# A two-layer hybrid attention backbone in fp32: the second score product of two head groups over all 128 array rows, with half of key's low part zero

## The chip, the cores and the metric

The kernel runs on one core of one Trainium2 chip. The metric is the device time of one launch in microseconds (us), the median of several runs. Less is better.

## What is computed

Two layers; each normalises 256 context tokens and 512 latent tokens of width 1024, projects them with one wide input matrix, and runs three head groups beside each other: neighbourhood attention (N, 8 heads of 64), latent attention with compressed query and key (M, 8 heads of 96) and differential attention (D, 4 heads, each with two softmax maps of 64). Every branch is gated, projected, merged and projected once more.

```python
s = jnp.einsum('bqhd,bkhd->bhqk', q, k).astype(jnp.float32) * scale      # M
s = jnp.einsum('bqhmd,bkhmd->bhmqk', q, k).astype(jnp.float32) * scale   # D
s_lat = jnp.einsum('bnqhd,bnkhd->bhnqk', qr, kb).astype(jnp.float32) * NA_SCALE + bias  # N, window
s_ctx = jnp.einsum('bnqhd,bkhd->bhnqk', qr, k_ctx).astype(jnp.float32) * NA_SCALE       # N, context
```

Everything is fp32. The kernel makes each fp32 product out of products of a high part `hi` (rounded to fp32r) and the rest `lo = x - hi`: `hi*hi + hi*lo + lo*hi`.

## The kernel before

`mixer` (L867) runs a layer as 12 steps in the order `DMNDMNDMNDMN`; each step projects one pair of heads of the kind named and computes the attention of the pair projected in the step before. Beside them stand work units with no hurry: gate products (`zgate` and `gm`, in the PSUM tile `fl`) and the modulation products (`ada_rows`, L230). The instructions of all this are put in order, engine by engine, by a scheduler that goes by the priorities in `PRI` and by its own times for the instructions, so TensorE's queue mixes score products of one pair with the projections of the next and with gate work, and each engine takes its queue strictly from the front.

**Projection of N and D pairs.** `proj_nd` (L398) computes q, k and v of two 64-wide heads `m = 0, 1` for tiles of 128 tokens (`mm3`, L115 to L117, in PSUM tile `pj`), normalises, and transposes (L451). Head 0 then lies on partitions 0 to 63 and head 1 on 64 to 127 (`halves`). For each head it keeps `q[m]`, 128 partitions with the high part of q in the head's own half and q's low part in the other half (L461, L462); `k[m]`, 128 partitions with the high part of k in the own half, which a DMA copies into the other half (L468); and the low part of k, `kl`, a tile of 128 partitions by 768 tokens in which head 0 has the upper and head 1 the lower 64 partitions. `kl` is written by VectorE in `split` (L127, D) or `gsplit` (L131, N); its tag has one buffer, and each projection of an N or D pair takes the tile anew.

**Scores of N and D.** A score tile takes two products (L470): `q[m]` by `k[m]` over 128 rows, which gives `qhi*khi + qlo*khi` at once, and `q[m][half]` by `kl[half]` over the 64 rows of the head, which gives `qhi*klo`:

```python
out["ops"] = lambda m, q0, k0, w: [(q[m][:, q0:q0 + P], k[m][:, k0:k0 + w]),
                                   (q[m][halves[m], q0:q0 + P], kl[halves[m], k0:k0 + w])]
```

`scores` (L690) issues the two one after the other: for D's latent queries over 512 and then 256 keys, 64 times in all (two layers, four pairs, two groups of 256 queries, two blocks of 128, two maps), and for context queries of D and N over 256 keys, 32 times in layer 0. `pair_scores` (L731), for latent N queries, issues for 256 context keys and again for 256 window keys the first products of both heads and then the second products of both: 8 products per call, 32 calls. M's scores use L690 too, with three products over 96 rows and no half tile.

**After the scores.** All scores go through one PSUM tile `sc` of 1024 columns (one buffer). VectorE takes the maximum (L796 for D), ScalarE the exponential (L694), after which `sc` is free again; N adds a bias first (L732). The probabilities are transposed (L680, L720) and multiplied with v (L851, L810).

Of the kernel before, what the change touches and what calls it, by code (L numbers as in the profile page):

```python
# [8 lines left out]
F32R = mybir.dt.float32r  # L9
# [5 lines left out]
P = 128  # L15
# [4 lines left out]
NTOK = CTX + SEQ  # L20
# [28 lines left out]
def f(ap):  # L49
    return ap.bitcast(F32)  # L50


class Mixer:
# [112 lines left out]
        nc.vector.tensor_scalar(out, ss, inv, EPS, ALU.mult, ALU.add)  # L166
        nc.gpsimd.tensor_tensor(out, out, self.nhalf[:, :cols], ALU.pow)  # L167

    # ---------------------------------------------------------------- setup
    def setup(self):  # L170
        nc, io = self.nc, self.io
        cc = self.cpool.tile([P, KT, 2], F32, name="cc")
        nc.sync.dma_start(cc, io["cc"])
        th = self.cpool.tile([P, KT, 2], F32, name="cth")
        nc.scalar.activation(th, cc, AF.Tanh, scale=0.5)
        nc.vector.scalar_tensor_tensor(th, th, 1.0, cc, ALU.add, ALU.mult)
        self.sT = self.cpool.tile([P, KT, 32], F32, name="sT")
        nc.gpsimd.memset(self.sT, 0.0)
        nc.vector.tensor_scalar(self.sT[:, :, 0:2], th, 0.5, None, ALU.mult)
        self.L = [self.layer_params(l) for l in range(DEPTH)]  # L180
# [124 lines left out]
            else:  # L305
                self.bg.pop(0)()

    # ---------------------------------------------------------------- h
    def norm_tile(self, pool, xt):
        nc = self.nc  # L310
        junk = pool.tile([P, D], F32, tag="junk", bufs=1, name=self.n("junk"))
        ss = self.lpool.tile([P, 1], F32, tag="ssx", bufs=6, name=self.n("ssx"))
        nc.scalar.activation(junk, xt, AF.Square, accum_out=ss)
        self.rstd(ss, ss, 1.0 / D, 1)
        nc.vector.tensor_scalar(xt, xt, ss, None, ALU.mult)
# [58 lines left out]
                nc.gpsimd.tensor_scalar(hi, tmp, 1.0, 0.0, ALU.mult, ALU.add)  # L374
                nc.vector.tensor_tensor(lo, tmp, f(hi), ALU.subtract)

    # ---------------------------------------------------------------- projections
    def proj_tok(self, ps, ws, t):
        for k in range(KT):
            a = [self.h[j][:, k, t * P:(t + 1) * P] for j in range(2)]  # L380
            self.mm3(ps, a, ws[k], k == 0, k == KT - 1)
# [16 lines left out]
    def proj_nd(self, l, kind, pr, pool, br):  # L398
        nc, io, Lp = self.nc, self.io, self.L[l]
        ws = self.units(io["w_qkv"][l, (0 if kind == "N" else 4) + pr])  # L400
        q, k = self.qks(pool), self.qks(pool)
        kl = pool.tile([P, NTOK], F32R, tag="kl", name=self.n("kl"))
        halves = (slice(0, 64), slice(64, 128))
        V = [pool.tile([P, 3, 256], F32R, tag="V", name=self.n("V")) for _ in range(2)]
        for tp in range(3):
            qks = []
            for t in (2 * tp, 2 * tp + 1):
                kv = l == 1 and t < 2
                o = P if kv else 0
                ng = 2 if kv else 4  # L410
                ps = self.pj()
                self.proj_tok(ps[:, o:384], [(a[:, o:], b[:, o:]) for a, b in ws], t)
                qn = pool.tile([P, 384], F32, tag="qn", name=self.n("qn"))
                one = self.ONE
                if one:
                    nc.scalar.copy(qn[:, o:], ps[:, o:384])
                    ps = qn
                self.vwrite(kind, V[t // 3][:, t % 3, :], ps[:, 256:384], one)
                v4 = lambda x: x[:, o:256].rearrange("p (a b) -> p a b", b=64)
                ss = pool.tile([P, 4], F32, tag="ss", name=self.n("ss"))  # L420
                r = ss[:, :ng].unsqueeze(2).to_broadcast([P, ng, 64])
                if kind in self.COPY or one:
                    if not one:
                        nc.scalar.copy(qn[:, o:256], ps[:, o:256])
                    sq = pool.tile([P, 256], F32, tag="sq", name=self.n("sq"))
                    nc.scalar.activation(sq[:, o:256], ps[:, o:256], AF.Square)
                    raw = qn
                else:
                    nc.scalar.activation(qn[:, o:256], ps[:, o:256], AF.Square)
                    sq, raw = qn, ps  # L430
                nc.vector.tensor_reduce(ss[:, :ng], v4(sq), AX.X, ALU.add)
                if kind == "D":
                    q3 = qn[:, o:256].rearrange("p (a m b) -> p a m b", m=2, b=64)
                    na = ng // 2
                    if t < 2:
                        nc.vector.tensor_tensor(q3, q3, br["G"][:, 2 - na:2].unsqueeze(2).to_broadcast([P, na, 2, 64]), ALU.mult)
                    else:
                        C, S = br["C"][:, t - 2], br["S"][:, t - 2]
                        t2 = pool.tile([P, 2, 2, 64], F32, tag="t2", name=self.n("t2"))
                        for x, y in ((0, 32), (32, 0)):  # L440
                            nc.gpsimd.tensor_tensor(t2[:, :, :, x:x + 32], q3[:, :, :, y:y + 32], S[:, :, x:x + 32].unsqueeze(2).to_broadcast([P, 2, 2, 32]), ALU.mult)
                        nc.vector.tensor_tensor(q3, q3, C.unsqueeze(2).to_broadcast([P, 2, 2, 64]), ALU.mult)
                        nc.vector.tensor_tensor(q3, q3, t2, ALU.add)
                self.rstd(ss[:, :ng], ss[:, :ng], 1.0 / 64, ng)
                nc.vector.tensor_tensor(v4(qn), v4(raw), r, ALU.mult)
                qks.append(qn)
            kv = l == 1 and tp == 0
            pt = self.pj()
            for i, qn in enumerate(qks):
                for j in ((1,) if kv else (0, 1)):  # L450
                    nc.tensor.transpose(pt[:, j * 256 + i * P:j * 256 + (i + 1) * P], qn[:, j * P:(j + 1) * P], self.ident)  # L451
            c = slice(tp * 256, tp * 256 + 256)
            if self.PF:
                pf = pool.tile([P, 512], F32, tag="pf", name=self.n("pf"))
                o = 256 if kv else 0
                (nc.scalar.copy if self.PF == "a" else nc.vector.tensor_copy)(pf[:, o:], pt[:, o:])
                pt = pf
            p3 = pt.rearrange("p (a t) -> p a t", a=2)
            for m, (own, oth) in enumerate((halves, halves[::-1])):
                if not kv:  # L460
                    nc.scalar.copy(q[m][own, c], p3[own, 0])  # L461
                    nc.vector.tensor_tensor(q[m][oth, c], p3[own, 0], f(q[m][own, c]), ALU.subtract)  # L462
                if kind == "N":
                    self.gsplit(k[m][own, c], kl[own, c], p3[own, 1], Lp["g"][own, 0:1])
                else:
                    self.split(k[m][own, c], kl[own, c], p3[own, 1])
        for m, (own, oth) in enumerate((halves, halves[::-1])):
            nc.sync.dma_start(f(k[m][oth, :]), f(k[m][own, :]))  # L468
        out = dict(V=V)
        out["ops"] = lambda m, q0, k0, w: [(q[m][:, q0:q0 + P], k[m][:, k0:k0 + w]),  # L470
                                           (q[m][halves[m], q0:q0 + P], kl[halves[m], k0:k0 + w])]
        if kind == "N":
            Vs = br["pool"].tile([P, 3, 256], F32R, tag="Vs", name=self.n("Vs"))
            nc.sync.dma_start(f(Vs[0:64, 0, :]), f(V[0][64:128, 2, :]))
            nc.sync.dma_start(f(Vs[0:64, 1:3, :]), f(V[1][64:128, 0:2, :]))
            nc.sync.dma_start(f(Vs[64:128, :, :]), f(V[1][0:64, :, :]))
            out["Vs"] = Vs
            out["bias"] = []
            for ty in range(3):
                bt = br["pool"].tile([P, 2, 256], F32, tag="bias", name=self.n("bias"))  # L480
                nc.sync.dma_start(bt, self.biasd[l][ty][2 * pr:2 * pr + 2].rearrange("h p k -> p h k"))
                out["bias"].append(bt)
        return out
# [166 lines left out]
        out["ops"] = ops  # L650
        return out

    # ---------------------------------------------------------------- attention
    def attn(self, l, kind, pr, a, zs, pool, ud):
        for grp in (self.GRP if l == 0 else (1, 2)):
            self.attn_group(l, kind, a, zs, pool, ud[self.BI[kind], pr], grp)
# [197 lines left out]
        nc.scalar.copy(tmp[mine, :], o[other, 0:256])  # L854
        nc.vector.tensor_tensor(u[mine, :], o[mine, 0:256], tmp[mine, :], ALU.add)  # L855

    # ---------------------------------------------------------------- layer
    POOLS = dict(pt2=1, th=1, qn=2, sq=2, t2=2, c2=2, c3=2, kr=2, krt=2, mss=2, ssr=2, ss=2)
    BUFS = dict(pf=1, mr=1, qk=6, kl=1, V=5, P=3, pt4=4, pt2=2, zs=2, ut=3, sq=1, ss=4, qn=3, st=3, t2=1, r0=2, th=1, c2=2, c3=1, mss=4, krt=2, Vs=1, bias=1, kr=1, ssr=1)
    BI = {"N": 0, "M": 1, "D": 2}  # L860
# [6 lines left out]
    def mixer(self, l):  # L867
# [4 lines left out]
        pool = _Pool(ps, self.BUFS, self.POOLS)  # L872
        gms = list(range(24))
        ada = [(0, 4), (0, 5), (1, 2), (1, 0), (1, 3), (1, 1)] if l == 0 else [(1, 4), (1, 5)]
        self.base = tc.cur_priority
        br = {"D": self.dtab, "N": dict(pool=pool), "M": None}
        prev = None
        seen = dict(D=0, M=0, N=0)
        for step, kind in enumerate(self.ORDER[l]):
# [53 lines left out]
        for n in range(KT):  # L933
# [4 lines left out]
            for c0, w in self.cols(l):  # L938
                c = slice(c0, c0 + w)
# [228 lines left out]
```

## Time and profile before

| | |
|---|---|
| median of 3 runs | 2018.39 us (2012.0 to 2019.07) |
| span of the profiled execution, first to last instruction | 2015.7 us |
| TensorE matmul busy | 1962.4 us, 97% of the span |
| VectorE / ScalarE / GpSimd busy | 60% / 47% / 38% |
| TensorE's granted clock, mean | 0.990 of full speed |

The profiled execution's own time is given by its span alone; what lies around the span in a run isn't listed for it. The median of the runs is 2.7 us above that span, and the span lies between the fastest and the slowest of the runs.

In a timeline, a matmul's row gives its start and a modelled duration. Matmuls overlap, so what one costs TensorE's queue is the distance from its start to the next row's start, not its duration. PE is TensorE's matmul, DVE VectorE, ACT ScalarE, POOL GpSimd, SP the queue that issues transfers. "64*128" in a row of TensorE is rows by columns of the array in use.

### The profile page before, as it was taken

The numbers are of one execution on the slowest core, as the hardware profiler recorded it, in microseconds if no ns is written. First come the engines' busy times: TensorE is split into PE (matmuls) and PEld (weight loads), VectorE is DVE, ScalarE is ACT, GpSimd is POOL, SyncE is SP. The second block draws the span as 40 slices with busy tenths as digits, with TensorE's granted clock in tenths as the row PEclk, the third lists the DMA queues.
The fourth block names the chain that finished last, engine by engine and source line by source line (L and its number), as shares of the span: only waits on it lengthen the run. The fifth ranks groups of instructions, "written<-read, shape, count | busy, mean of one in ns | idle before, by whom it ended". The sixth has DMA issues, their size and how long they took to land.

```text
span 2015.7 us, 33972 instructions
## 1 busy us (share of the span) xinstructions
PE 1962.4 (97%) x11650; PEld 1745.5 (87%) x11650; DVE 1217.9 (60%) x2808; ACT 938.1 (47%) x2422; POOL 762.3 (38%) x1053
## 2 busy tenths in 40 slices
PE   6999999999999999999999999999999999999998
PEld 4988998998888988989999988897698789889878
DVE  5556667555765555646663465667667466666763
ACT  4445455444544544435532354555455345555531
POOL 3333233323423322332355454334344234343353
PEclk9999999999999999999999999999999899999999
DMA  9553113333434333332655243323513322432663
GB/s 320 185 157 123 41 56 104 110 120 111 124 110 145 90 100 119 98 108 70 199 175 178 92 129 125 110 66 91 163 54 93 112 72 81 119 126 59 189 188 112
DMA packets 172600, 243.28 MB, mean 121 GB/s; under 512 B 22710, under 2 KB 127560, under 8 KB 172428
## 3 DMA queue, kind: packets, MB, share of 16 engines
q1 hardware_dynamic: 172428, 241.12, 38.3%
q8 instruction: 92, 1.51, 0.3%
q14 instruction: 80, 0.66, 0.1%
HBM read 190.38 MB, written 44.49 MB: 117 GB/s over the span
## 4 chain that ended last, share of the span: by engine, by line
PE 90%; DVE 4%; DMA 2%; ACT 1%; issue 1%; POOL 1%; SPq 0%; DVEq 0%; ACTq 0%; POOLq 0%
PE pj L115 11%; PE pj L117 11%; PE pj L116 11%; PE fl L115 10%; PE fl L116 9%; PE fl L117 9%; PE sc L690 9%; PE bk L851 5%; PE bk L680 4%; PE fl L230 2%; PE sc L731 2%; PE bk L810 2%; PE pj L640 1%; PE pj L451 1%; DVE w L127 1%
## 5 line engine op out<-in xcount | busy, mean ns | idle before, releaser
L122 ACT CAST w<-ws 128x384 fp32r<-128x384 f32 (+3 forms) x520 | 237.2, 474 | 268.4 <-PE fl L116 159.2
L127 POOL TENSOR_TENSOR w<-ws,w 128x384 fp32r<-128x384 f32 (+3 forms) x260 | 241.9, 936 | 312.6 <-ACT w L122 301.7
L115 PE MATMUL fl<-h,w 128*128 128x384 f32 (+1 forms) x864 | 316.5, 366 | 4.1 <-DVE zs L392 2.7
L115 PE MATMUL pj<-w,h 128*128 128x384 f32 (+2 forms) x944 | 314.5, 336 | 2.0 <-DVE kl L127 1.1
L117 PE MATMUL fl<-h,w 128*128 128x384 f32 (+1 forms) x864 | 312.8, 362 | 0.0
L116 PE MATMUL fl<-h,w 128*128 128x384 f32 (+1 forms) x864 | 312.8, 362 | 0.0
L116 PE MATMUL pj<-w,h 128*128 128x384 f32 (+2 forms) x944 | 309.6, 330 | 0.0
L117 PE MATMUL pj<-w,h 128*128 128x384 f32 (+2 forms) x944 | 307.5, 330 | 1.0 <-POOL h L127 0.6
L127 DVE TENSOR_TENSOR w<-ws,w 128x384 fp32r<-128x384 f32 (+2 forms) x260 | 177.4, 686 | 74.4 <-ACT w L122 67.0
L167 POOL TENSOR_TENSOR ss<-ss,nhalf 128x4 f32<-128x4 f32 (+1 forms) x144 | 142.8, 992 | 179.2 <-DVE ss L166 166.3
L694 ACT ACTIVATE P<-sc,st 128x768 f32<-128x768 f32 (+1 forms) x192 | 159.5, 832 | 104.7 <-DVE st L796 39.1
L741 POOL TENSOR_SCALAR P<-P,st 128x512 f32<-128x512 f32 (+1 forms) x128 | 107.8, 845 | 256.0 <-DVE st L737 216.7
L684 DVE TENSOR_TENSOR pt<-bk,pt 128x512 fp32r<-128x512 f32 (+1 forms) x256 | 147.8, 586 | 64.9 <-ACT pt L683 62.7
L117 PEld LDWEIGHTS pj<-w,h 128*128 128x128 f32 x944 | 177.0, 189 | 9.6 <-issue 5.9
L115 PEld LDWEIGHTS pj<-w,h 128*128 128x128 f32 x944 | 177.6, 189 | 8.8 <-issue 3.8
L116 PEld LDWEIGHTS pj<-w,h 128*128 128x128 f32 x944 | 178.2, 189 | 5.7 <-issue 5.0
L115 PEld LDWEIGHTS fl<-h,w 128*128 128x128 f32 x864 | 164.4, 190 | 18.3 <-DVE zs L392 4.9
L117 PEld LDWEIGHTS fl<-h,w 128*128 128x128 f32 x864 | 164.1, 190 | 13.1 <-DVE w L127 0.5
L683 ACT CAST pt<-bk 128x512 fp32r<-128x512 f32 (+1 forms) x256 | 126.9, 506 | 104.3 <-PE bk L680 101.8
L116 PEld LDWEIGHTS fl<-h,w 128*128 128x128 f32 x864 | 164.2, 190 | 11.0
L690 PE MATMUL sc<-qk,qk 96*128 96x512 f32 (+3 forms) x592 | 153.2, 353 | 3.0 <-DMA qk<-qk 3.0
L680 PE MATMUL bk<-cst,P 128*128 128x128 f32 x832 | 130.1, 274 | 2.7 <-DVE u L855 1.8
(236 smaller groups left out, 3995.9 us busy)
## 6 DMA issues: line engine op xcount, KB each, us to landing
ws<-in_w_qkv SPq DMA_DIRECT2D x128, 192.0 KB
ws<-in_w_gm SPq DMA_DIRECT2D x96, 192.0 KB
aw<-in_w_ada SPq DMA_DIRECT2D x64, 256.0 KB
ct<-cqd SPq DMA_DIRECT2D x40, 384.0 KB
ct<-ckd SPq DMA_DIRECT2D x48, 256.0 KB
ws<-in_w_z SPq DMA_DIRECT2D x48, 192.0 KB
thd<-th SPq DMA_DIRECT2D x48, 192.0 KB
ws<-in_w_br SPq DMA_DIRECT2D x48, 192.0 KB
```

Source lines behind the costliest of these rows:

```text
L115: mm(out, a[0], b[0], start=first, stop=False)
L116: mm(out, a[0], b[1], start=False, stop=False)
L117: mm(out, a[1], b[0], start=False, stop=last)
L122: nc.scalar.copy(hi, src)
L127: (nc.gpsimd if le == "g" else nc.vector).tensor_tensor(lo, src, f(hi), ALU.subtract)
L167: nc.gpsimd.tensor_tensor(out, out, self.nhalf[:, :cols], ALU.pow)
L680: nc.tensor.transpose(pt[:, i * P:(i + 1) * P], src[:, (b0 + i) * P:(b0 + i + 1) * P], self.ident)
L683: nc.scalar.copy(h, v)
L684: nc.vector.tensor_tensor(lo, v, f(h), ALU.subtract)
L690: mm(s[:, d0:d0 + w], x, y, start=i == 0, stop=i == len(ops) - 1)
L694: nc.scalar.activation(p, src, AF.Exp, bias=st[:, m:m + 1], accum_out=st[:, 2 + m:3 + m])
L741: nc.gpsimd.tensor_scalar(p, p, st[:, 4 + m:5 + m], 0.0, ALU.mult, ALU.add)
```

## The change

The low part of k gets a tile of its own for each layer, `self.kl`, of 128 partitions by 2 heads by 768 tokens. At the start of the layer GpSimd sets the half that doesn't belong to the head to zero, in two memsets of 64 partitions by 768. Projections write the head's own half, as before, and the second product takes all 128 rows of `q[m]` and of `kl[:, m]`: q's low part, in the other half, meets zeros.

```diff
 def proj_nd(self, l, kind, pr, pool, br):
-        kl = pool.tile([P, NTOK], F32R, tag="kl", name=self.n("kl"))
+        kl = self.kl
...
                 if kind == "N":
-                    self.gsplit(k[m][own, c], kl[own, c], p3[own, 1], Lp["g"][own, 0:1])
+                    self.gsplit(k[m][own, c], kl[own, m, c], p3[own, 1], Lp["g"][own, 0:1])
                 else:
-                    self.split(k[m][own, c], kl[own, c], p3[own, 1])
+                    self.split(k[m][own, c], kl[own, m, c], p3[own, 1])
...
         out["ops"] = lambda m, q0, k0, w: [(q[m][:, q0:q0 + P], k[m][:, k0:k0 + w]),
-                                           (q[m][halves[m], q0:q0 + P], kl[halves[m], k0:k0 + w])]
+                                           (q[m][:, q0:q0 + P], kl[:, m, k0:k0 + w])]
...
 def mixer(self, l):
         br = {"D": self.dtab, "N": dict(pool=pool), "M": None}
+        self.kl = pool.tile([P, 2, NTOK], F32R, tag="kl", name=f"kl{l}")
+        for m in range(2):
+            self.nc.gpsimd.memset(f(self.kl[64 - 64 * m:128 - 64 * m, m]), 0.0)
```

Each engine issues the same instructions as before, apart from the four memsets on GpSimd. Their order shifts in places, because the tile is no longer taken anew by each pair and the scheduler plans again. Three places follow; a number behind a tile's name tells one tile of that name from another.

GpSimd at the start of layer 0, with the change: `h` is the normalised input, `mss` the mean squares of M's compressed inputs.

```order
L346 TENSOR_TENSOR h_1_109<-htmp_444,h_0_108 128x256
L346 TENSOR_TENSOR h_1_109<-htmp_460,h_0_108 128x512
L879 MEMSET kl_484 64x768 x2
L167 TENSOR_TENSOR mss_577<-mss_577,nhalf 128x1
L167 TENSOR_TENSOR mss_617<-mss_617,nhalf 128x1
```

The two memsets stand between the last piece of `h` and the first of the `mss` rows; those rows follow each other directly before. In layer 1 the pair of memsets stands between a piece of `h` and a weight's low part in the same way.

VectorE where layer 0 goes from its first N pair to its second D pair (step 3): `sc` with `bias` is the bias add on N's scores, `kl<-pj,qk` writes the low part of the D pair's keys. Before:

```order
L855 TENSOR_TENSOR u_3308<-bk_3381,ot_3394 64x256 [waits DMAHW0_49,Activation_49]
L855 TENSOR_TENSOR u_3308<-bk_3397,ot_3410 64x256 [waits Activation_49]
L732 TENSOR_TENSOR sc_3454<-sc_3454,bias_3174 128x2x256 [waits DMAHW1_49,PE_49]
L127 TENSOR_TENSOR kl_3572<-pj_3649,qk_3571 64x256
L127 TENSOR_TENSOR kl_3572<-pj_3744,qk_3571 64x256
```

With the change:

```order
L684 TENSOR_TENSOR pt_3311<-bk_3364,pt_3310 128x4x128 [waits Activation_49]
L127 TENSOR_TENSOR kl_484<-pj_3744,qk_3572 64x256 [waits PE_49]
L732 TENSOR_TENSOR sc_3421<-sc_3421,bias_3173 128x2x256 [waits PE_49]
L684 TENSOR_TENSOR pt_3313<-bk_3375,pt_3312 128x4x128 [waits Activation_49]
L501 TENSOR_TENSOR V_3574<-pj_3798,V_3574 128x128 [waits Activation_49]
```

Before, the D pair's first write of `kl` stands behind the last bias add of the N pair. Now it stands ahead of the bias add of the block before that one, and waits for TensorE itself.

TensorE in a later D pair of layer 0, around two successive score tiles `sc` of one block of queries. Before:

```order
L690 MATMUL sc_6604<-qk_6179,qk_6178 128x512
L690 MATMUL sc_6604<-kl_6180,qk_6178 128x512
L690 MATMUL sc_6604<-qk_6179,qk_6178 128x256
L690 MATMUL sc_6604<-kl_6180,qk_6178 128x256
L720 MATMUL bk_6563<-cst,P_6555 128x128 x4
L810 MATMUL bk_6570<-pt_6538,V_6181 128x256
L115 MATMUL fl_7247<-h_0_108,w_7229 128x384
```

With the change:

```order
L690 MATMUL sc_6602<-qk_6178,qk_6177 128x512
L690 MATMUL sc_6602<-kl_484,qk_6177 128x512
L690 MATMUL sc_6602<-qk_6178,qk_6177 128x256
L690 MATMUL sc_6602<-kl_484,qk_6177 128x256
L720 MATMUL bk_6561<-cst,P_6553 128x128 x4
L810 MATMUL bk_6568<-pt_6536,V_6179 128x256
L690 MATMUL sc_6610<-qk_6178,qk_6177 128x512
```

Before, twenty gate products (`fl`) and one transpose stood between these rows and the next score tile; with the change the next score tile follows after five short products.

## Rows read from the trace of the kernel before

**Rows 1.** The page: busy time per engine, and the chain that ended last

```profile
PE 1962.4 (97%) x11650; PEld 1745.5 (87%) x11650; DVE 1217.9 (60%) x2808; ACT 938.1 (47%) x2422; POOL 762.3 (38%) x1053
PE 90%; DVE 4%; DMA 2%; ACT 1%; issue 1%; POOL 1%; SPq 0%; DVEq 0%; ACTq 0%; POOLq 0%
```

**Rows 2.** Groups of TensorE by line, shapes apart: busy us, mean ns | idle before

```profile
L690 PE MATMUL sc<-kl,qk 64*128 64x256 f32 x96 | 36.8, 383 | 0.0
...
L690 PE MATMUL sc<-kl,qk 64*128 64x512 f32 x64 | 32.1, 501 | 0.0
...
L731 PE MATMUL sc<-kl,qk 64*128 64x256 f32 x128 | 25.6, 384 | 0.0
```

**Rows 3.** Timeline of TensorE, a D score tile: start us, us, instruction

```profile
185.03 0.39 PE L690 MATMUL sc<-qk,qk 128*128 128x512 f32 x1
185.35 0.50 PE L690 MATMUL sc<-kl,qk 64*128 64x512 f32 x1
185.78 0.38 PE L690 MATMUL sc<-qk,qk 128*128 128x256 f32 x1
186.09 0.39 PE L690 MATMUL sc<-kl,qk 64*128 64x256 f32 x1
186.41 0.44 PE L115 MATMUL fl<-h,w 128*128 128x384 f32 x1
186.69 0.33 PE L116 MATMUL fl<-h,w 128*128 128x384 f32 x1
186.86 0.34 PE L117 MATMUL fl<-h,w 128*128 128x384 f32 x1
```

**Rows 4.** Timeline of TensorE, value products and an M score tile

```profile
211.77 2.31 PE L810 MATMUL bk<-pt,V 128*128 128x256 f32 x18
213.92 1.21 PE L690 MATMUL sc<-qk,qk 96*128 96x512 f32 x6
214.96 0.34 PE L117 MATMUL pj<-w,h 128*128 128x384 f32 x1
215.14 0.34 PE L115 MATMUL pj<-w,h 128*128 128x384 f32 x1
```

**Rows 5.** Timeline of TensorE, one call of N's latent scores

```profile
285.68 0.48 PE L731 MATMUL sc<-qk,qk 128*128 128x256 f32 x2
286.09 0.38 PE L731 MATMUL sc<-kl,qk 64*128 64x256 f32 x2
286.40 0.50 PE L731 MATMUL sc<-qk,qk 128*128 128x256 f32 x2
...
287.15 0.44 PE L451 MATMUL pj<-cst,qn 128*128 128x128 f32 x2
```

**Rows 6.** Timeline of TensorE, three pairs of products of D's context queries

```profile
145.02 0.28 PE L690 MATMUL sc<-qk,qk 128*128 128x256 f32 x1
145.23 0.38 PE L690 MATMUL sc<-kl,qk 64*128 64x256 f32 x1
...
146.80 0.45 PE L115 MATMUL fl<-h,w 128*128 128x384 f32 x1
147.08 0.34 PE L116 MATMUL fl<-h,w 128*128 128x384 f32 x1
```

**Rows 7.** Who waited for whom, TensorE: us in total, times, longest us

```profile
PE pj L115 <- DVE kl L127: 1.1, 1, 1.1
```

**Rows 8.** Timelines of ScalarE and TensorE behind the D score tile of group 3

```profile
187.51 0.91 ACT L694 ACTIVATE P<-sc,st 128x768 f32<-128x768 f32 x1 [1.89 <-DVE st L796]
...
191.10 0.40 PE L690 MATMUL sc<-qk,qk 128*128 128x512 f32 x1
```

**Rows 9.** GpSimd: the nearest memset by tile, and its timeline as layer 0 starts

```profile
L74 POOL MEMSET neg<- x1: 311/311/311, 0.8 to 0.8; 128x256 f32 x1
...
49.84 1.33 POOL L346 TENSOR_TENSOR h<-htmp,h 128x512 fp32r<-128x512 f32 x1 [1.34 <-ACT h L344]
54.33 1.76 POOL L167 TENSOR_TENSOR mss<-mss,nhalf 128x1 f32<-128x1 f32 x3 [3.16 <-DVE mss L166]
```

## The prediction

> **What bounds the kernel.** I read the page first: matmuls keep TensorE busy for 97% of the span, VectorE, ScalarE and GpSimd for 60%, 47% and 38%, and 90% of the chain that ended last is TensorE's own work [rows 1]. What leaves TensorE's queue is therefore time, as long as nothing else is late. A busy share says nothing about how full the array is, so next come the groups of TensorE with the shapes apart. There, 288 products take only 64 rows of the array (96, 64 and 128 of them), and one over 256 columns is marked with 383 or 384 ns, over 512 with 501 [rows 2]. These durations overlap, so last I read the distances from start to start in the timeline.
>
> In a D score tile the starts lie at 185.03, 185.35, 185.78 and 186.09, and the gate product behind at 186.41: 1.38 us for two products of 512 and two of 256 columns; the next product is late too, 0.28 us instead of 0.17 [rows 3]. In an M score tile, which goes to the same `sc` and has 96 rows, three products of 512 and three of 256 columns take 1.04 us (the row counts all six and names the first one's shape), and behind them the distance is the usual 0.18 [rows 4]. The difference lies at every change between 128 and 64 rows: each product on either side of one starts some 0.1 to 0.2 us later than in a run of equal shapes.
>
> **Which form decides.** A 96-row product costs no more than one of full rows. The reading that fits all groups is that the array must be empty before it goes from a full-height to a half-height tile, or back. The Trainium skill, TensorEngine Tiling (Array Packing), Key Properties, says it so: changing the tiling mode drains the engine. The trace agrees, by the 1.38 us against two thirds of 1.04.
>
> **The sum, part by part.** All of it is distances on TensorE's queue, which is the path.
>
> 1. *D's latent scores, 64 tiles.* From 185.03 to 186.86 the queue does four score products and two gate products in 1.83 us [rows 3]. With full rows everywhere I take M's price: two thirds of 1.04, 0.69, plus two gate products at 0.18, 1.05 us [rows 4]. Gain 0.78 x 64 = 49.9 us.
> 2. *Context scores of D and N, 32 pairs of products.* Three pairs and one gate product take from 145.02 to 147.08, 2.06 us [rows 6]. Full products of 256 columns follow each other at (213.92 - 211.77) / 18 = 0.119 us [rows 4], so six and a gate product take 0.90. Gain 1.16 per three pairs, 0.39 x 32 = 12.4 us.
> 3. *N's latent scores, 32 calls of 8 products.* A call takes from 285.68 to 287.15, 1.47 us [rows 5]. Eight full products at 0.119 take 0.95. Gain 0.52 x 32 = 16.6 us. Here the change also gives something up: the second products of the two heads lie in different halves of the array, and both take only 0.31 us, 286.09 to 286.40 [rows 5]. Afterwards they stand one behind the other, which the 0.95 counts. The Trainium skill, TensorEngine Tiling (Array Packing), When to Use Tiling, speaks against the change: contractions of 64 or fewer rows are to be packed as two half tiles. By that rule alone padding would cost 64 more products of 0.119, 7.6 us, instead of bringing 16.6, and the sum of the three parts would be 54.7; I go by the rows, because in them the two changes of height cost more than the pairing saves.
>
> These make 78.9 us. Upper end: each call of N may also give back a late product behind it, as in D (0.1 x 32 = 3.2 us), and the one wait on a write of `kl`, 1.1 us [rows 7], may go: 83 us.
>
> 4. *Zero rows.* They cost TensorE nothing, since 96 rows cost what 128 do; VectorE writes as many partitions as before.
> 5. *Four memsets.* The nearest row is one of 256 columns, 0.31 us [rows 9]; 768 columns make 0.93, a pair 1.9 us per layer. In layer 0 GpSimd then idles 3.16 us before the `mss` rows [rows 9], which cover it. In layer 1 I don't know the cover: 0 to 1.9 us, and I take 0. Without cover M's first transposes would start that much later.
> 6. *The order.* At the seam from N to D, VectorE's first write of `kl` now stands ahead of a bias add and waits for TensorE. The waits for tokens that N's later blocks don't read end earlier, so PSUM tiles come free earlier; I count nothing. In a later D pair the next score tile follows after five short products, about 0.6 us. A score tile is free when the exponential has read it, 187.51 + 0.91 = 188.42, some 2.0 us behind its last product [rows 8]; so this place stalls by about 1.4 us. Elsewhere the next tile of the pair comes at 191.10 [rows 8], 2.7 us after the release. That distance consists of work that the change leaves alone, so the chain behind the scores is not squeezed where the order holds.
> 7. *What doesn't follow.* A tenth of the chain isn't TensorE's [rows 1], and in those stretches a shorter queue brings nothing: 78.9 x 0.1 = 7.9 us, an estimate. The 1.4 us of point 6 I count as part of it.
>
> Net gain 78.9 - 7.9 = 71 us. The profiled span is 2015.7, so the new span should be 1944.7. The median of the runs stands 2.7 us above that span, and I carry the same distance: **1947 us**, 3.5% less.
>
> **Rivals.**
>
> *Other engines become the bound.* TensorE gets ahead of weight splits and softmax steps, and waits take back 25 to 55 us, say half of 78.9. For it: VectorE would be busy 1217.9 of some 1945 us, 63%, and unevenly; one order place is tighter. Against: before, TensorE hardly waits on any of them, and the slack between score tiles holds filler that stays. Time 2018 - 40 = 1978 us; chance 0.14.
>
> *Only D gains.* If the pairing of half tiles is worth more in N than one call shows (in calls with other work between, the changes of height may be hidden), padding only adds 64 products of 0.119 there, and point 3 becomes a loss of 7.6 us: 49.9 + 12.4 - 7.6 = 54.7, less a tenth, 49. Time 2018 - 49 = 1969 us. The packing rule of the Trainium skill named in point 3 would have it so. The 1.47 us against 0.95 speak against it; chance 0.05.
>
> *The change doesn't do what it says.* If the late starts come from score operands or from `sc`, not from the array's height, the full-row second product keeps its distance, and N loses its pairs, 7.6 us: 2026 us, no change to speak of. M's scores have the same `sc` and the same 128-column operand at 1.04 us per six, which speaks against it; chance 0.04.
>
> *Slower, by the seam.* VectorE takes its queue in order. If the early `kl` write waits for TensorE while TensorE waits for something behind that write, each of the six seams from N to D becomes a stall. It decides only above 79 + 10 us, some 15 us at each seam, since the gain has to be eaten first; 20 us each would give 2018 - 71 + 120 = 2067. The wait that exists today there is 1.1 us, once [rows 7]. Chance 0.03.
>
> **How the numbers follow.** The forecast with its own ends (gain 55 to 90 us) has 0.74. The fast end is 83 us plus the spread of the runs shown, 7 us: 2018 - 90 = 1928. The slow end takes in most of the first rival and all of the second: 1984. About 0.5%, 10 us, is what a measurement of this kernel can tell from no change. Faster: forecast and the first two rivals, 0.93. The same: the third, and a little of the fourth that stays small, 0.04. Slower: 0.03.
>
> **What would show it.** Right: no group of 64 rows in TensorE's list, about 1.38 us shrunk to 0.7 in a D score tile and 1.47 to about 0.95 in an N call, the product behind at its usual 0.18; busy time of the other engines as before; TensorE's waits longer by under 10 us in all. Wrong: score products of full rows still 0.3 us apart (third rival); TensorE's waits on ScalarE and VectorE up by 25 us or more (first); a wait of `kl` on VectorE's queue with PSUM tiles held behind it (fourth).

## The result, and the profile after

The changed kernel takes **1949.18 us** (median of four runs, 1946.06 to 1951.95), the kernel before 2015.77 (four runs, 2012.0 to 2019.07): ratio 0.9666, 95% interval 0.9642 to 0.969, so 3.3% faster, 66.6 us. The forecast was 1947 in a range of 1928 to 1984. The profiled execution's own time is 1946.06 and its span 1944.3 us.

The page of the kernel after, busy time and chain, answers to [rows 1]:

```profile
PE 1882.9 (97%) x11650; PEld 1731.5 (89%) x11650; DVE 1213.2 (62%) x2808; ACT 936.3 (48%) x2422; POOL 766.0 (39%) x1057
PE 87%; DVE 4%; DMA 4%; ACT 2%; issue 1%; POOL 1%; SPq 0%; DVEq 0%; ACTq 0%; POOLq 0%
```

TensorE is 79.5 us less busy with the same 11650 products. It stands idle for 1944.3 - 1882.9 = 61.4 us, before for 2015.7 - 1962.4 = 53.3. The other engines' busy times hardly differ.

The groups of TensorE with shapes apart, kernel after, answer to [rows 2]:

```profile
L731 PE MATMUL sc<-kl,qk 128*128 128x256 f32 x128 | 26.8, 288 | 0.0
...
L690 PE MATMUL sc<-kl,qk 128*128 128x256 f32 x96 | 26.3, 281 | 0.0
...
L690 PE MATMUL sc<-kl,qk 128*128 128x512 f32 x64 | 25.1, 393 | 0.0
```

The same 288 products with `kl`, now all over 128 rows: over twice the rows each is marked shorter, 281 to 288 ns instead of 383 and 384, and 393 instead of 501. At a change of height a product's mark takes in the load of its weights, which starts with it there (last section); a shorter mark doesn't mean that a product computes faster.

The D score tile of [rows 3], timeline of TensorE, kernel after:

```profile
186.91 0.40 PE L690 MATMUL sc<-qk,qk 128*128 128x512 f32 x1
187.14 0.39 PE L690 MATMUL sc<-kl,qk 128*128 128x512 f32 x1
187.37 0.28 PE L690 MATMUL sc<-qk,qk 128*128 128x256 f32 x1
187.49 0.28 PE L690 MATMUL sc<-kl,qk 128*128 128x256 f32 x1
187.60 0.28 PE L117 MATMUL pj<-w,ct 128*128 128x256 f32 x1
```

From 186.91 to 187.60, 0.69 us instead of 1.38, and the product behind is followed at 187.72, the usual distance for 256 columns.

A call of N's latent scores, timeline of TensorE, kernel after, answers to [rows 5]; it stands behind transposes (L680), as the call of [rows 5] does:

```profile
278.22 0.38 PE L680 MATMUL bk<-cst,P 128*128 128x128 f32 x2
278.35 0.48 PE L731 MATMUL sc<-qk,qk 128*128 128x256 f32 x2
278.67 0.40 PE L731 MATMUL sc<-kl,qk 128*128 128x256 f32 x2
...
279.39 0.38 PE L451 MATMUL pj<-cst,qn 128*128 128x128 f32 x2
```

It takes 1.04 us instead of 1.47. The forecast was 0.95.

One view the prediction did not read says directly what went: the waits of the weight loads (PEld), where "issue" is a wait for nothing else that the profile shows. Columns: us in total, times, longest. Kernel before:

```profile
PEld sc L690 <- issue: 38.1, 137, 1.7
...
PEld sc L731 <- issue: 0.6, 3, 0.2
```

The kernel after has neither row; all "issue" rows of the weight loads together fall from 77.6 us in 212 waits to 35.9 in 68. N's calls (L731) hardly show in it, so the view finds D's and the context's changes of height and not all of the loss.

**How exactly 71 us were met.** The two profiled spans differ by 71.4 us, where the forecast's sum said 71. That is too good. The mean granted clock is 0.990 in the profile before and 0.993 in the one after, and at equal clock the gain is smaller: a run of the kernel after at 0.990 has a span of 1949.6 against the 2015.7 of the profile before, 66.1 us less, and 1944.3 at 0.993 stands against 2008.7 to 2010.2 in three runs of the kernel before at 0.993, 64.4 to 65.9. I take 65 us as the size of the effect. The 2.7 us from span to median were luck of the same kind: every run on record lies 1.7 to 1.9 us above its own span, and the measured median stands 4.9 us above the profiled span, because the fastest of the four runs was profiled.

### The profile page after: what moved, and what is told of

The parts are those of the page before. It is cut to its first block, busy times and chain, and to the rows that moved or that the text cites. A ratio compares the mean times of both kernels' runs of the same rounds, so it can differ in the third digit from the quotient of the medians.

```text
span 1944.3 us, 33969 instructions
## 1 busy us (share of the span) xinstructions
PE 1882.9 (97%) x11650; PEld 1731.5 (89%) x11650; DVE 1213.2 (62%) x2808; ACT 936.3 (48%) x2422; POOL 766.0 (39%) x1057
## 4 chain that ended last, share of the span: by engine, by line
PE 87%; DVE 4%; DMA 4%; ACT 2%; issue 1%; POOL 1%; SPq 0%; DVEq 0%; ACTq 0%; POOLq 0%
PE pj L117 11%; PE pj L115 11%; PE pj L116 11%; PE fl L115 10%; PE fl L116 9%; PE fl L117 9%; PE sc L690 6%; PE bk L851 4%; PE bk L680 4%; PE fl L230 2%; PE bk L810 2%; PE sc L731 1%; DMA aw<-in_w_ada 1%; PE pj L640 1%; PE pj L451 1%
## 5 line engine op out<-in xcount | busy, mean ns | idle before, releaser
L684 DVE TENSOR_TENSOR pt<-bk,pt 128x512 fp32r<-128x512 f32 (+1 forms) x256 | 147.8, 586 | 61.2 <-ACT pt L683 58.6
L690 PE MATMUL sc<-qk,qk 96*128 96x512 f32 (+3 forms) x592 | 143.5, 337 | 3.8 <-DMA qk<-qk 2.9
L680 PE MATMUL bk<-cst,P 128*128 128x128 f32 x832 | 130.2, 274 | 4.7 <-DVE pt L684 2.4
```

The source lines that it names most:

```text
L680: nc.tensor.transpose(pt[:, i * P:(i + 1) * P], src[:, (b0 + i) * P:(b0 + i + 1) * P], self.ident)
L684: nc.vector.tensor_tensor(lo, v, f(h), ALU.subtract)
L690: mm(s[:, d0:d0 + w], x, y, start=i == 0, stop=i == len(ops) - 1)
```

## The experiments

Two theories. **Height:** the time goes at every change between 128 and 64 rows, so it returns with the half rows, follows the number of changes, and D and N add up. **Tile and order:** the tile that is kept through the layer, the earlier token releases and the new order bring a good part of it. A third question came from the prediction's rival, whether N gains at all. Ratios are to the kernel before in the same batch (medians 2012.96 for the first four kernels, 2013.53 for the last two).

| kernel | median us | ratio, 95% interval | TensorE busy | idle | granted clock |
|---|---|---|---|---|---|
| e1, half rows again, tile and memsets kept | 2019.36 | 1.0032, 1.0017 to 1.0047 | 1974.0 | 50.7 | 0.985 |
| e2, full rows for D alone | 1963.45 | 0.9736, 0.9705 to 0.9767 | 1906.7 | 56.8 | 0.993 |
| e3, full rows for N alone | 1999.99 | 0.9928, 0.9905 to 0.995 | 1943.9 | 58.0 | 0.989 |
| e4, e1 with D's products grouped | 1994.87 | 0.9906, 0.988 to 0.9931 | 1941.0 | 56.1 | 0.988 |
| e5, e2 with N's products grouped | 1957.84 | 0.9727, 0.9707 to 0.9748 | 1898.2 | 57.7 | 0.991 |
| e6, the changed kernel, grouped as e4 | 1952.22 | 0.97, 0.9676 to 0.9725 | 1887.0 | 61.4 | 0.991 |

Busy time, idle time (the span less the busy time) and mean clock are those of the profiled run; busy times at different clocks compare only roughly. Line numbers shift by a few lines in e2 to e6.

**e1: the height alone is taken back.**

```diff
-                                           (q[m][:, q0:q0 + P], kl[:, m, k0:k0 + w])]
+                                           (q[m][halves[m], q0:q0 + P], kl[halves[m], m, k0:k0 + w])]
```

> The changed kernel with its tile for key's low part, its zeros and its memsets, but the second product takes only the 64 rows of the head again. If the array's height is the whole cause, all of the gain goes: 2016 us (2009 to 2023), matmul busy time back at about 1962 us, D score tiles back at 1.38 us. If the tile that is kept through the layer, or the order that comes with it, brings part of the gain, the time lies between: about 1980 us for half. TensorE's idle time (53 us before, 61 us after the change) tells by the way whether the new order alone makes it wait more: about 61 us if so, about 53 us if the idle time grew because TensorE got faster.

2019.36 us, the whole gain is gone. Timeline of TensorE, a D score tile of e1:

```profile
182.44 0.40 PE L690 MATMUL sc<-qk,qk 128*128 128x512 f32 x1
182.77 0.50 PE L690 MATMUL sc<-kl,qk 64*128 64x512 f32 x1
183.20 0.38 PE L690 MATMUL sc<-qk,qk 128*128 128x256 f32 x1
183.51 0.38 PE L690 MATMUL sc<-kl,qk 64*128 64x256 f32 x1
183.82 0.87 PE L680 MATMUL bk<-cst,P 128*128 128x128 f32 x6
```

1.38 us again, and the weight loads of `sc` (L690) wait as before, 37.1 us in 136 waits. In e1's trace 98% of TensorE's 11650 products stand at the same place of the queue as in the changed kernel. So the lasting tile and the order it brings give nothing. The 6 us above the kernel before lie mostly in the clock: its mean is 0.989 over the ten runs of e1 and 0.991 over the fifteen of the kernel before, and 0.0023 between the unrounded means, of 2016 us, is some 4.7 us. The busy time of 1974.0 us, 12 above the expected 1962, is mostly clock as well: while busy, TensorE was at the lower level for 58.6 us in e1's profile and for 37.1 in that of the kernel before, which makes some 10 us (an estimate, by the 0.43 and 0.23 us of the last section). Idle time is 50.7 us here: the changed kernel's 61.4 don't come with the tile or the memsets, which e1 has too.

**e2 and e3: D alone, N alone.** e2 has, in `proj_nd` (e3 the same with "N"):

```diff
+        hs = (slice(0, P), slice(0, P)) if kind == "D" else halves
...
-                                           (q[m][:, q0:q0 + P], kl[:, m, k0:k0 + w])]
+                                           (q[m][hs[m], q0:q0 + P], kl[hs[m], m, k0:k0 + w])]
```

> Full rows for D alone, 64 rows for N. By the sum of the prediction N's latent scores (16.6 us) and N's half of the context pairs (6.2 us) are lost, less a tenth: 1949 + 20 = 1969 us (1963 to 1976). If the pairing of two half tiles is worth more in N than the changes of height cost, N is no loss: 1949 us or less.

> Full rows for N alone, 64 rows for D. By the sum D's latent scores (49.9 us) and D's half of the context pairs (6.2 us) are lost, less a tenth: 1949 + 50 = 1999 us (1992 to 2006). If N is no gain: 2016 us or more. If the two groups don't add up (one hides behind the other), what this run and the run with D alone gain against before does not make the whole gain of 67 us.

D alone brings 2.64%, N alone 0.72%; together 3.36%, and the whole change brings 3.34%. At equal clock (0.992) e2 runs 48 to 51 us below the kernel before and e3 13, in spans. e2 lies at the fast end of its range, 1963.45 us with 1963 to 1976 expected, and e3 within 1 us of what was expected. e3 shows that N gains although it gives up the pairs of half tiles: "only D gains" is out.

**e4: half rows, but fewer changes.** Back to half rows; a D tile's two first products stand together, then its two second ones, so a tile has two changes of height instead of four. Context scores have one pair of products in each call of `scores`, so they stay as they were. The work is that of e1.

```diff
+            all_ops = [a["ops"](m, q0, k0, w) for _, k0, w in segs]
...
+            for i in range(n):
+                for (d0, k0, w), ops in zip(segs, all_ops):
+                    mm(s[:, d0:d0 + w], *ops[i], start=i == 0, stop=i == n - 1)
```

> 64 rows as in the run with half rows, but D's score tile issues both first products (512 and 256 columns) and then both second ones: two changes of height instead of four, the same number of half-row products. If each change of height costs, 0.78 / 4 = 0.195 us, two fewer in each of 64 tiles give 25 us, less a tenth 22: about 1994 us, and a D tile of 1.38 us becomes about 1.0. If each half-row product is what costs, nothing changes against the run with half rows: 2016 us.

1994.87 us, as expected to a microsecond. Timeline of TensorE, e4 (each score row counts two products and names the first one's shape):

```profile
188.31 0.51 PE L696 MATMUL sc<-qk,qk 128*128 128x512 f32 x2
188.75 0.61 PE L696 MATMUL sc<-kl,qk 64*128 64x512 f32 x2
189.29 0.44 PE L115 MATMUL fl<-h,w 128*128 128x384 f32 x1
```

0.98 us for the tile. Two changes fewer save 0.40 us of 1.38, and all four fewer save 0.78 with the late product behind: 0.2 us for one change. The waits of the weight loads of `sc` shrink with the changes, e4:

```profile
PEld sc L696 <- issue: 17.3, 72, 0.3
```

Other weight loads wait longer there: all "issue" rows together make 67.3 us in 200 waits, against 77.6 in the kernel before. The view points at the changes but does not measure what they cost.

**e6: the grouping with full rows.** Is it the grouping itself, not the changes saved, that helps e4? The edit is e4's, on the changed kernel.

> The changed kernel, all products over full rows, with D's products grouped as in the run that grouped them over 64 rows. It tells whether the grouping gained there because it halves the changes of height, or because the regrouped order is better in itself. If changes of height are the cause, there are none left to save: 1949 us (1944 to 1955). If the order is better in itself, some 20 us less: 1929 us.

1952.22 us, 0.97 against 0.9666 with overlapping intervals: without changes of height to save, the grouping brings nothing.

**The same order, another height.** By names and shapes, and apart from the height, TensorE's queue in e2's trace is that of e1 at all 11650 places; e3's is that of the changed kernel, and e6's is that of e4. Between the two of a pair only the height differs, in D and its context scores, and in the last pair in N's too. The medians differ by 55.9 us (e1 to e2), 50.8 (e3 to the changed kernel) and 42.7 (e4 to e6), the clock not taken out. So the order of TensorE's work is no rival explanation.

**e5: N's pairs kept, but together.** e2, with the four first products of an N call together and then its four half-tile products, two changes of height instead of four.

```diff
-            for d0, k0 in ((0, 0), (256, CTX + BAND[qt - 2])):
-                for i, xy in enumerate(zip(*(a["ops"](m, qt * P, k0, 256) for m in range(2)))):
-                    for m, (x, y) in enumerate(xy):
...
+            for i in range(2):
+                for d0, k0 in ((0, 0), (256, CTX + BAND[qt - 2])):
+                    for m in range(2):
...
```

> Full rows for D, 64 rows for N as in the run with D alone; but a call of N's latent scores issues its four first products and then its four second ones, in two pairs that lie side by side in the array: two changes of height instead of four, the pairing kept. A call cost 1.47 us with four changes, of which two pairs of half tiles and four full products are 6 x 0.119 = 0.71, so a change costs (1.47 - 0.71) / 4 = 0.19 us; with two changes a call takes 1.09. Against the run with D alone (1963 us) that gives 0.38 x 32 = 12 us, less a tenth 11: 1952 us (1947 to 1958). If the pairing brings nothing but in the two heads' order before, or the half-row product is what costs, nothing changes: 1963 us.

Timeline of TensorE, e5, a call behind transposes:

```profile
282.00 0.72 PE L733 MATMUL sc<-qk,qk 128*128 128x256 f32 x4
282.65 0.50 PE L733 MATMUL sc<-kl,qk 64*128 64x256 f32 x4
283.08 0.44 PE L451 MATMUL pj<-cst,qn 128*128 128x128 f32 x2
```

1.08 us, against 1.47 before and 1.04 with full rows. The call is as short as expected. The time, 1957.84 us, lies at the slow end of its range (1947 to 1958) and only 5.6 us below e2, and the intervals of the two overlap, so the times alone don't show a gain. TensorE's busy time fell by 8.5 us, of the 12.5 that 32 calls would give (0.39 x 32), and its idle time rose by 0.9. Most of the missing 4 us is clock: while busy, TensorE was at the lower level for 32.2 us in e5's profile and for 26.7 in e2's, which makes some 2.5 us (an estimate, as in e1). That e5 stays behind the changed kernel doesn't speak against the packing: e5 keeps N's context pairs at 64 rows, 6.2 us in the prediction's sum. In the calls themselves, packing half tiles and filling them with zeros come out nearly alike once the changes are few: 0.04 us a call, 1.3 us in 32, too little for these times to tell.

No run beat the changed kernel.

## Why the prediction was right, point by point

**Which form decides.** Right. The price is that of a change of height (e4, e1), not of the product, the tile or `sc`. That the array must be empty first is a reading of the starts; the price has a second part that the prediction does not name, the load of the weights (last section).

**Point 1, D's latent tiles: right to 2 us.** 0.69 us forecast for the tile, 0.69 in the one shown, and the usual distance behind it. In e1 and e2, whose queues are alike, all 64 tiles, each up to the start of the second product behind it, take 106.7 and 58.6 us: 48 us, not 49.9.

**Point 2, context scores: right for the products, not for what follows.** The timeline of all engines, kernel after, at the place of [rows 6] (PEld is the weight load; in brackets idle time before, and what ended it):

```profile
146.78 0.28 PE L690 MATMUL sc<-kl,qk 128*128 128x256 f32 x1
...
147.17 0.19 PEld L115 LDWEIGHTS fl<-h,w 128*128 128x128 f32 x1 [0.32 <-ACT th L993]
147.17 0.44 PE L115 MATMUL fl<-h,w 128*128 128x384 f32 x1
...
147.45 0.33 PE L116 MATMUL fl<-h,w 128*128 128x384 f32 x1
```

The six products follow each other at the forecast 0.12 us, from 146.19 on. But the gate product behind now comes too early for its PSUM tile, which ScalarE's tanh still reads: 1.26 us up to 147.45 instead of the forecast 0.90. Of 1.16 us gained 0.36 turn into a wait. This is point 7 in one place.

**Point 3, N's latent calls: the term that was mis-sized.** I put a call that stands behind transposes, 1.47 us, against eight products that follow one another, 0.95. Timeline of TensorE, calls behind a value product (L851), kernel before:

```profile
292.95 0.41 PE L731 MATMUL sc<-qk,qk 128*128 128x256 f32 x2
...
294.35 0.62 PE L851 MATMUL bk<-pt,V 128*128 128x256 f32 x3
```

Kernel after:

```profile
285.12 0.41 PE L731 MATMUL sc<-qk,qk 128*128 128x256 f32 x2
285.37 0.40 PE L731 MATMUL sc<-kl,qk 128*128 128x256 f32 x2
...
286.08 0.53 PE L851 MATMUL bk<-pt,V 128*128 128x256 f32 x3
```

Behind transposes the first full products are late in both kernels: in the kernel after 278.35 to 278.67 is 0.32 us for two, and 285.12 to 285.37, behind a value product, 0.25; in the kernel before 285.68 to 286.09 [rows 5] is 0.41, and 292.95 to 293.29 is 0.34. Like with like, 1.47 became 1.04 behind transposes, and behind a value product 1.40 (292.95 to 294.35, kernel before) became 0.96 (285.12 to 286.08, kernel after). So the gain is 0.43 or 0.44 a call, 14 us in all instead of 16.6. (The 22 calls of either trace that stand undivided at the full clock have means of 1.44 and 1.01 us.) With D's 48 the sum is 74 instead of 78.9. The measured fall of TensorE's busy time, 79.5, holds the better clock too: 0.003 of about 2000 us is 6 us, which leaves 74.

**Point 4, zero rows: right,** by the groups above.

**Point 5, memsets: cheaper than estimated, and covered in layer 0.** GpSimd as layer 0 and layer 1 start, kernel after (two pieces of its timeline):

```profile
50.60 1.33 POOL L346 TENSOR_TENSOR h<-htmp,h 128x512 fp32r<-128x512 f32 x1 [1.34 <-ACT h L344]
53.42 1.52 POOL L879 MEMSET kl<- 64x768 f32 x2 [1.49 <-DVE htmp L345]
55.16 1.59 POOL L167 TENSOR_TENSOR mss<-mss,nhalf 128x1 f32<-128x1 f32 x3 [0.21 <-DVE kr L540]
...
1147.88 1.52 POOL L879 MEMSET kl<- 64x768 f32 x2
```

A pair takes 1.52 us, not 1.9. In layer 0 it lies in the gap ahead of the `mss` rows, as forecast, although it first waits 1.49 us for VectorE. The `mss` rows come at 55.16 instead of 54.33 [rows 9], 0.83 us late, but the piece of `h` ahead of the memsets is 0.76 us late already (50.60, before 49.84), so less than 0.1 us is left for the pair. In layer 1 GpSimd's next instruction follows directly behind it; what the 1.5 us cost there no run shows alone. By e1, which is hardly slower than its clock explains, tile and memsets together cost a microsecond or two at most.

**Point 6, the order: right in size, half of it by another wait.** The place where two score tiles of a D pair come close, timeline of TensorE, kernel after:

```profile
544.82 0.60 PE L720 MATMUL bk<-cst,P 128*128 128x128 f32 x4
546.10 0.39 PE L810 MATMUL bk<-pt,V 128*128 128x256 f32 x1 [0.68 <-ACT pt L722]
547.06 0.50 PE L690 MATMUL sc<-qk,qk 128*128 128x512 f32 x1 [0.57 <-ACT P L694]
```

From 544.82 to 547.06 five short products take 2.24 us instead of about 0.6, a stall of 1.6 us; 1.4 were forecast, all for ScalarE's exponential. That wait is only 0.57 us; the 0.68 before it is one for the transposed probabilities (`pt`), which the prediction did not count.

**Point 7, what doesn't follow: the size about right, in part by luck.** 7.9 us forecast; idle time rose by 8.1, and 74 less the 65 at equal clock is 9. The forecast took a tenth because a tenth of the old chain wasn't TensorE's. What the runs show are longer waits as TensorE gets faster: with the same order of its work, idle time goes from 50.7 us (e1) to 56.8 (e2), from 58.0 (e3) to 61.4 (the changed kernel) and from 56.1 (e4) to 61.4 (e6). That this made just about a tenth of the gain was not derived. It is spread out. Waits of TensorE for modulation weights (`aw`), kernel before (us in total, times, longest):

```profile
PE fl L230 <- DMA aw<-in_w_ada: 3.7, 1, 3.7
```

Kernel after:

```profile
PE fl L230 <- DMA aw<-in_w_ada: 5.8, 5, 3.2
```

That is 2.1 of the 8.1 us; the chain's share of transfers went from 2% to 4%.

**The rivals.** Other engines becoming the bound would have shown as 25 us more of waits; it was 8. "Only D gains" fell with e3, "doesn't do what it says" with the groups by shape and e1. The fourth rival, the seam from N to D, shows no wait of TensorE on `kl`. The prediction took the wait of [rows 7] for one at the seam, but it stands in the projection of the first D pair, ahead of every N pair, at 113.66 us in the kernel before and here in the kernel after (timeline of TensorE):

```profile
114.88 0.41 PE L115 MATMUL pj<-w,h 128*128 128x384 f32 x1 [1.08 <-DVE kl L127]
```

## What to carry to other kernels

Where TensorE is the path, read distances from start to start and look for products of another height among full ones: here each change cost 0.2 us, more than a 256-column product of full rows (0.12). Fill the missing rows with zeros, or put products of one height together: both helped in D; in N grouping made the call as short as filling did, but its gain in time was not clear of the noise. Filling was the simpler. When a difference is made from two rows, take both from the same neighbourhood (behind transposes or not) and the same granted clock.

## What the runs showed of the hardware

**The weight load loses its lead at a change of height.** Weight loads in the timeline, the D score tile of the kernel before [rows 3]:

```profile
184.91 0.19 PEld L690 LDWEIGHTS sc<-qk,qk 128*128 128x128 f32 x1
185.35 0.18 PEld L690 LDWEIGHTS sc<-kl,qk 64*128 64x128 f32 x1 [0.25 <-issue]
185.78 0.19 PEld L690 LDWEIGHTS sc<-qk,qk 128*128 128x128 f32 x1 [0.24 <-issue]
186.09 0.18 PEld L690 LDWEIGHTS sc<-kl,qk 64*128 64x128 f32 x1
```

Kernel after:

```profile
186.91 0.19 PEld L690 LDWEIGHTS sc<-kl,qk 128*128 128x128 f32 x1
187.14 0.19 PEld L690 LDWEIGHTS sc<-qk,qk 128*128 128x128 f32 x1
187.37 0.19 PEld L690 LDWEIGHTS sc<-kl,qk 128*128 128x128 f32 x1
```

With full rows each load starts with the product before its own: the product at 187.14 has its weights loaded from 186.91 on, beside the product of 186.91. At a change of height load and product start together, at 185.35, 185.78 and 186.09. The Trainium skill, TensorE: Matmul & The Clock Gate, The mechanism (in the part on packing small matmuls), says in its list of what overlaps that weight loads overlap running products only where the row groups differ; ahead of that list the same section also lets loads into a background weight buffer go ahead. The trace disagrees with the list: loads over the same full rows overlap, 0.12 to 0.23 us ahead, and those at a change of height do not.

So the rows split the 0.2 us of a change in two. Behind a full product of 512 columns whose weights were loaded ahead, the half-height product starts after 0.32 us (185.03 to 185.35) instead of 0.23 (186.91 to 187.14): 0.09 us in which the array finishes, by the prediction's reading. Behind a product that starts together with its load the next one of the same height is late by another 0.11 us, 0.28 instead of 0.17 [rows 3]. A product between two changes pays both: 0.43 us for 512 columns (185.35 to 185.78).

**Slower runs are runs at a lower granted clock.** The longest stretch at the lower level in these two profiles lies at a wait for modulation weights in layer 1. The granted clock in stretches of 5 us, TensorE alone, kernel before (stretch, length, busy with count, clock, share and GB/s of transfers):

```profile
1560.00:1565.00 5.00, 1.66 (x5) 0.94 0.90 282
1565.00:1570.00 5.00, 5.00 (x19) 0.50 0.04 9
...
1580.00:1585.00 5.00, 5.00 (x20) 0.85 0.15 43
```

Kernel after:

```profile
1510.00:1515.00 5.00, 1.52 (x6) 0.74 0.91 272
1515.00:1520.00 5.00, 5.00 (x18) 0.50 0.36 99
1520.00:1525.00 5.00, 5.00 (x25) 0.73 0.00 0
```

After a wait of 3.70 us (up to 1563.34) the kernel before is at half of full speed, 1.2 GHz instead of 2.4, for some 17 us although TensorE is busy throughout; the kernel after for some 10, from 1512.4 on, inside its wait of 3.15 us (up to 1514.11). In the kernel before, gate products of 512 columns follow each other at 0.43 us in that stretch (1578.10 to 1578.53) and at 0.23 behind it (1581.74 to 1581.97), so a little under half of the time at the lower level is lost. Over the fifteen runs of the kernel before in the first batch the mean clock runs from 0.988 (spans 2016.4 to 2018.7) to 0.994 (2009.0 to 2009.7). This one stretch doesn't explain the spread: it is 17 of 38 us at the lower level in the profile before, 10 of 26 in the one after, but 14 of 63 in e1's. Whether an earlier transfer of these weights would help was not tried.
